# Four blocks of the up projection as seven products of quarter matrices in place of eight

## The chip, the core and the metric

The kernel runs on one core of a Trainium2 chip. The metric is the device time of one run in microseconds (us); less is better. The engines are named as the profile names them: PE (TensorE, matrix products) with PEld (the loading of its weights), DVE (VectorE), ACT (ScalarE), POOL (GpSimd) and SP (SyncE, which here issues DMA transfers). SBUF is the on-chip memory, PSUM the banks in which PE sums its products.

## The reference, cut to what matters

A block of a network: 512 tokens of 1024 values go through two mixers (a recurrent one and a sparse attention), a feed-forward stage with a short convolution, and a gated projection. All is float32. The change is in the feed-forward stage:

```python
def conv_ffn(h, w_up, conv_w, conv_b, w_down):
    u = h @ w_up                                  # [512,1024] @ [1024, 2*2048]
    gate, val = jnp.split(u, 2, axis=-1)
    gate = lax.conv_general_dilated(gate, ...) + conv_b   # width 3 along the tokens, each column by itself
    return (jax.nn.silu(gate) * val) @ w_down     # [512,2048] @ [2048,1024]
...
x = x + conv_ffn(rms_norm(x, ln2_g[i]), w_up[i], conv_w[i], conv_b[i], w_down[i])
```

`rms_norm` multiplies each token's row by one over its root mean square and each column by a gain.

## The kernel before, in words

Every large product is made of three products: both operands are split into a high part (rounded to the type fp32r, on ACT, tile names that end in h) and a low part (value minus high part, on DVE, names that end in l), and PE adds high x high, high x low and low x high in one PSUM bank (`gemm`, L443 to L452).

The feed-forward stage has 16 blocks f of 128 hidden columns. A block is two jobs: `wu{f}0` makes the gate rows, `wu{f}1` the value rows, each [128 columns x 512 tokens] over 1024 inputs in eight steps of 128, so 24 matmuls of 128x512 a job and 48 a block. The job's weight (128x1024) comes by a DMA into a tile that ends in r, ACT copies the high part (L166), DVE subtracts (L167). The class `Stream` works the list of jobs down: when a job begins it splits the next job's weight (`prepare(1)`). Raw, high and low weight tiles have two buffers each, and a new one is filled when the work that read the old one is done. The order of the instructions on each engine follows from data: an engine works its list in order, and the list is laid out by a scheduler from the program and the waits.

The inputs x2h and x2l are scaled by the gain alone. One over the root mean square of each token (the row `n2rb`) is multiplied in where the result leaves PSUM: `up_evac` (L1135 to L1153) makes zg from the gate's bank (DVE, times n2rb), three instructions of the convolution cv (ACT, DVE, DVE), the silu (ACT), zv from the value's bank (DVE, times n2rb), zv times cv (DVE), and the split of the result u (ACT high, DVE low). POOL has one 128x2 memset per block. After the 16 blocks the down projection reads U, whose four tiles hold four blocks each.

`xturn` is a tile of the down stage, `mixa`, `XH`, `XL` and `B16` are tags of large buffers that several stages use one after the other; `x2h` lies in XH and `x2l` in XL.

Of the kernel before, what the change touches and what calls it, by code (L numbers as in the profile page):

```python
# [19 lines left out]
NT = 4  # L20
# [38 lines left out]
C_G2, C_G3, C_GF = 0, 8, 16  # L59
C_CW, C_CB = 24, 72  # L60
# [8 lines left out]
def f32(ap):  # L69
    return ap.bitcast(F32)  # L70
# [3 lines left out]
def hybrid_block_kernel(ctx: ExitStack, tc: tile.TileContext, a, out):  # L74
    nc = tc.nc
    TE, VE, SE, GE = nc.tensor, nc.vector, nc.scalar, nc.gpsimd

    consts = ctx.enter_context(tc.tile_pool(name="consts", bufs=1))
    main = ctx.enter_context(tc.tile_pool(name="main", bufs=1))
    wpool = ctx.enter_context(tc.tile_pool(name="wpool", bufs=2))  # L80
# [20 lines left out]
    def pV(name):  # L101
        return bank("V", 1, 1, name)
# [7 lines left out]
    def t2k(name, dt=F32):  # L110
        return tmp.tile([128, 512], dt, tag="t2k", name=name)
# [37 lines left out]

    turn = [0]  # L150

    def load(name, src_ap, shape):
        raw = None
        if early[0]:
            turn[0] += 1
            if turn[0] % 6 < 4:
                raw = early[0][:, turn[0] % 6].rearrange("p (a b) -> p a b", a=shape[1])
        if raw is None:
            raw = wpool.tile(shape, F32, tag="raw", bufs=2, name=name + "r")
        nc.sync.dma_start(raw, src_ap)  # L160
# [21 lines left out]
    class Stream:  # L182


        def __init__(self):
            self.jobs, self.loaded, self.ready, self.cur, self.done = [], [], [], None, set()
            self.now, self.events, self.debt = 0.0, [], 0.0

        def add(self, name, src, shape, run):
            self.jobs.append((name, src, shape, run))  # L190

        def load(self, depth):
            while len(self.loaded) < depth and self.jobs:
                name, src, shape, run = self.jobs.pop(0)
                self.loaded.append((name, load(name, src, shape), shape, run))
                if name == "mv3":
                    early[0] = None

        def prepare(self, depth):
            while len(self.ready) < depth and (self.jobs or self.loaded):  # L200
                self.load(1)
                name, raw, shape, run = self.loaded.pop(0)
                self.ready.append((name, run, split(name, raw, shape)))

        def after(self, us, fn):
            self.events.append((self.now + us, len(self.events), fn))
# [49 lines left out]
    st = Stream()  # L256
# [211 lines left out]
    Q, vo, qk, X = {}, None, None, None  # L468
# [278 lines left out]
    mixa = main.tile([128, 2, 4, S], F32R, tag="mixa", name="mixa")  # L747
# [346 lines left out]
    x2h = main.tile([128, KB, S], F32R, tag="XH", name="x2h")  # L1094
    x2l = Halves("x2l")
# [5 lines left out]
    n2, n3 = {}, {}  # L1101

    def up_job(f, part):
        def run(wh, wl):
            ps = pW(f"pu{f}{part}")
            if f == 0:
                for k in range(KB):
                    triple(ps, wh, wl, k, x2h, x2l, k, k == 0, k == KB - 1)
                    yield 0.64
            else:  # L1110
                yield from gemm(ps, wh, wl, range(KB), x2h, x2l, range(KB))
            defer(n2, lambda: up_evac(f, part, ps, n2["rb"]))
        st.add(f"wu{f}{part}", a["w_up"][:, f, part], [128, KB, 128], run)

# [6 lines left out]
    def start_norm(norm, acc, name):  # L1121
        def stats():
            yc = rstd_stats(acc, name)
            if norm is n3:
                norm["yc"] = yc
                return
            st.after(T_NR, lambda: rows(yc))

        def rows(yc):
            norm["rb"] = rstd_rows(yc, name)  # L1130
            for fn in norm.get("pending", []):
                fn()
        st.after(T_NS, stats)

    def up_evac(f, part, ps, rb2):  # L1135
        if part == 0:
            zg = fpool.tile([128, S + 2], F32, name=f"zg{f}", tag="zg")
            GE.memset(zg[:, 0:2], 0.0)  # L1138
            VE.tensor_mul(zg[:, 2:S + 2], ps, rb2)  # L1139
            cw = lambda j: cols[:, C_CW + 16 * j + f:C_CW + 16 * j + f + 1]  # L1140
            cv = fpool.tile([128, S], F32, name=f"cv{f}", tag="cv")
            SE.activation(cv, zg[:, 2:S + 2], AF.Identity, scale=cw(2), bias=cols[:, C_CB + f:C_CB + f + 1])  # L1142
            VE.scalar_tensor_tensor(cv, zg[:, 1:S + 1], cw(1), cv, op0=ALU.mult, op1=ALU.add)  # L1143
            VE.scalar_tensor_tensor(cv, zg[:, 0:S], cw(0), cv, op0=ALU.mult, op1=ALU.add)  # L1144
            SE.activation(cv, cv, AF.Silu)  # L1145
            n2["cv"] = cv
# [134 lines left out]
    sa = pSa("pga")  # L1281
# [146 lines left out]
```

## Time and profile before

| | us |
|---|---|
| median of 3 runs (lowest to highest) | 629.54 (629.13 to 630.43) |
| the profiled run | 630.01 |
| its span, first to last instruction | 627.8 |
| PE busy in the span | 617.1 (98%) |
| DVE, ACT, POOL busy | 416.5 (66%), 315.9 (50%), 62.4 (10%) |
| granted TensorE clock, mean | 0.996 of full speed |

The chain that ended last is led by the last instructions of DVE (2% of the span); before them lies PE's work. The page's row of 40 slices shows PE at 9 tenths or more in all slices but the last. The feed-forward's up blocks begin at about 311 us. A duration in a row goes from the start of an instruction to its end; where instructions of an engine stand in a row, their starts are closer together than their durations, since one begins before the other has drained. The time that one costs its engine in a row is therefore read from start to start.

### The profile page before, as it was taken

The page shows a single profiled execution, that of the slowest core. Times are in us where ns is not written, and L with a number is a line of the kernel's source. Part 1 is how long each engine was busy: PE and PEld are TensorE (multiplying, and loading weights), DVE is VectorE, ACT ScalarE, POOL GpSimd, SP SyncE. Part 2 cuts the span into 40 slices and gives each one's busy share as a digit, 9 for nine tenths or more (in the row PEclk, how much of TensorE's full clock was granted, in tenths as well). Part 3 has the DMA queues.
Part 4 walks back from the last instruction along what each step waited for, and adds up shares of the span by engine and source line. Part 5 has one row for each costly group of instructions (what it writes and reads, how often), then busy time and mean ns, then how long its engine had stood idle before and what let it go on. Part 6 is the DMA issues. An engine that isn't in the chain of part 4 may idle for free. (4 is left out here: it accounts for less than half of the span.)

```text
span 627.8 us, 8441 instructions
## 1 busy us (share of the span) xinstructions
PE 617.1 (98%) x3021; PEld 500.7 (80%) x3021; DVE 416.5 (66%) x807; ACT 315.9 (50%) x663; POOL 62.4 (10%) x131
## 2 busy tenths in 40 slices
PE   9999999999999999999999999999999999999995
PEld 6888877777777777878888888888888888888784
DVE  6988757787777778882966665655556434345376
ACT  7455556677667766653744333334334223233254
POOL 0400009332333400000000000000000000000000
PEclk9999999999999999999999999999999999999998
DMA  8822136111221323022333322233333222534603
GB/s 304 306 64 70 36 103 157 42 37 66 68 68 34 132 71 101 34 69 67 101 101 100 102 86 90 92 101 101 101 101 101 96 89 85 165 103 138 185 14 135
DMA packets 23210, 63.04 MB, mean 100 GB/s; under 512 B 2744, under 2 KB 7736, under 8 KB 23100
## 3 DMA queue, kind: packets, MB, share of 16 engines
q1 hardware_dynamic: 21632, 59.93, 29.0%
q0 software_dynamic: 1248, 2.16, 1.5%
q8 instruction: 24, 0.39, 0.2%
q10 hardware_dynamic: 288, 0.41, 0.2%
q14 instruction: 18, 0.15, 0.1%
HBM read 56.72 MB, written 2.10 MB: 94 GB/s over the span
## 5 line engine op out<-in xcount | busy, mean ns | idle before, releaser
L808 POOL TENSOR_SCALAR E<-E,rr,sg 128x512 f32<-128x512 f32 (+3 forms) x54 | 38.3, 710 | 71.7 <-DVE rr L803 57.8
L1152 ACT ACTIVATE u<-zv 128x512 fp32r<-128x512 f32 x16 | 10.1, 634 | 45.0 <-DVE zv L1150 45.0
L837 DVE TENSOR_TENSOR pl<-pt,ph 128x512 fp32r<-128x512 f32 x40 | 27.2, 686 | 7.6 <-ACT ph L836 7.0
L1149 DVE TENSOR_TENSOR zv<-pu,n2rb 128x512 f32<-128x512 f32 x16 | 11.0, 691 | 31.0 <-PE pu L451 31.0
L836 ACT ACTIVATE ph<-pt 128x512 fp32r<-128x512 f32 x40 | 23.7, 600 | 15.4 <-PE pt L833 14.0
L1139 DVE TENSOR_TENSOR zg<-pu,n2rb 128x512 f32<-128x512 f32 x16 | 11.1, 692 | 26.0 <-PE pu L451 24.6
L833 PE MATMUL pt<-cols,E 128*128 128x128 f32 x160 | 26.4, 274 | 0.5 <-DVE E L808 0.4
L1138 POOL MEMSET zg<- 128x2 f32 x16 | 1.5, 99 | 244.0 <-DVE cv L1144 150.6
L1179 DVE TENSOR_TENSOR X<-pd,X 128x512 f32<-128x512 f32 x8 | 5.5, 692 | 29.6 <-PE pd L451 29.6
L833 PEld LDWEIGHTS pt<-cols,E 128*128 128x128 f32 x160 | 20.0, 140 | 6.3 <-DVE E L808 1.1
L1142 ACT ACTIVATE cv<-zg,cols 128x512 f32<-128x512 f32 x16 | 13.1, 817 | 20.1 <-DVE zg L1139 20.1
L1145 ACT ACTIVATE cv<-cv 128x512 f32<-128x512 f32 x16 | 10.1, 631 | 24.9 <-DVE cv L1144 24.9
L801 ACT ACTIVATE E<-s,nm 128x384 f32<-128x384 f32 (+2 forms) x48 | 22.1, 471 | 0.0
L841 PE MATMUL pv<-ph,V 128*128 128x512 f32 x40 | 18.9, 473 | 0.0
L1153 DVE TENSOR_TENSOR u<-zv,u 128x512 fp32r<-128x512 f32 x16 | 11.1, 692 | 10.5 <-ACT u L1152 10.5
L803 DVE RECIPROCAL rr<-rs 128x3 f32<-128x3 f32 x32 | 5.5, 172 | 16.9 <-ACT E L801 16.7
L843 PE MATMUL pv<-pl,V 128*128 128x512 f32 x40 | 16.5, 411 | 0.2 <-DVE pl L837 0.2
L791 DVE TENSOR_REDUCE nm<-s 128x2 f32<-128x768 f32 (+2 forms) x24 | 16.3, 680 | 0.0
L284 DVE TENSOR_TENSOR acc<-acc,sq 128x512 f32<-128x512 f32 x21 | 14.4, 684 | 0.1
L801 ACT ACTIVATE Ec<-s,nm 128x32 f32<-128x32 f32 x24 | 6.8, 283 | 13.5 <-DVE nm L791 10.4
L1144 DVE SCALAR_TENSOR_TENSOR cv<-zg,cols,cv 128x512 f32<-128x512 f32 x16 | 12.0, 751 | 0.5
L1143 DVE SCALAR_TENSOR_TENSOR cv<-zg,cols,cv 128x512 f32<-128x512 f32 x16 | 11.9, 746 | 0.2 <-issue 0.2
(1223 smaller groups left out, 2022.9 us busy)
## 6 DMA issues: line engine op xcount, KB each, us to landing
X<-in_xg SPq DMA_DIRECT2D x1, 2048.0 KB, 8.7
xo<-xturn SPq DMA_DIRECT2D x32, 64.0 KB, 2.0
wgr<-in_w_pg SPq DMA_DIRECT2D x4, 512.0 KB, 4.1
s1r<-in_w_s SPq DMA_DIRECT2D x3, 676.0 KB, 8.8
xT<-in_xg SPq DMA_DIRECT2D x3, 514.0 KB, 7.8
rawx<-in_w_mv SPq DMA_DIRECT2D x3, 512.0 KB, 6.5
Q<-hlq POOLq DMA_DIRECT2D x12, 128.0 KB, 3.1
out_y<-xo SPq DMA_DIRECT2D x3, 512.0 KB, 2.6
```

The lines of the kernel that those rows point to most:

```text
L284: return VE.tensor_add(acc[:, :n], acc[:, :n], sq[:, :n])
L791: VE.tensor_reduce(out=nm[:, 1:3], in_=sw, axis=AX.X, op=ALU.max, negate=True)
L801: SE.activation(e, p, AF.Exp, bias=nm[:, b:b + 1], accum_out=rs[:, b:b + 1])
L808: eng.tensor_scalar(e, e, rr[:, b:b + 1], sg[:, i, 3 * h + b:3 * h + b + 1], op0=ALU.mult, op1=ALU.mult)
L833: TE.transpose(pt[:, r * 128:(r + 1) * 128], Es[r][:, c0:c0 + 128], ident)
L836: SE.activation(ph, pt, AF.Copy)
L837: VE.tensor_sub(pl, pt, f32(ph))
L841: TE.matmul(pv, vs, ph, start=first, stop=False)
L843: TE.matmul(pv, vs, pl, start=False, stop=last)
L1142: SE.activation(cv, zg[:, 2:S + 2], AF.Identity, scale=cw(2), bias=cols[:, C_CB + f:C_CB + f + 1])
L1143: VE.scalar_tensor_tensor(cv, zg[:, 1:S + 1], cw(1), cv, op0=ALU.mult, op1=ALU.add)
L1144: VE.scalar_tensor_tensor(cv, zg[:, 0:S], cw(0), cv, op0=ALU.mult, op1=ALU.add)
```

## The change

Blocks 8, 9, 10 and 11 (`FAST`) are done by another formula. The product of a block, [2 x 128 columns] by [2 halves of the 1024 inputs] by [2 halves of the 512 tokens], is eight products of quarters; the changed kernel makes it of seven products of sums of quarters. Each is over 512 inputs in four steps and over 256 tokens: 12 matmuls of 128x256, so 84 a block.

- The sums of the inputs need inputs that are fully normalised: `scaled_input` makes xn (X times gain times n2rb), its high and low part xnh and xnl, one of eight pieces at a time while blocks 0 to 4 run, and POOL makes the sums tf (16 subtractions of 128x256). After block 4, `split_sums` splits them into th and tl. Blocks from 5 on read xnh and xnl, and no longer multiply by n2rb: zg is a copy by ACT, zv one DVE product less.
- The sums of the weights (`landed_b`) are made by POOL for each of the four blocks: four additions or subtractions of 128x512 into a tile `ws`, which has one buffer (the tag xturn). A block has four jobs: a (`wu{f}0`, gate weight, two products), b (`wu{f}s`, two sums), c (`wu{f}t`, two sums) and d (`wu{f}1`, half a weight, one product). So three splits of 128x1024 and one of 128x512 in place of two of 128x1024.
- The seven results are combined by a copy of ACT and seven additions of DVE over 256 columns. The convolution and the rest are as before, without n2rb.
- The four banks of blocks 8 and 10 are single tiles; blocks 9 and 11 take a two-bank tile (`pSa`) and two others.
- From before block 7 to the end of block 11 the weights are split two jobs ahead and loaded four ahead, and the raw tiles get two more buffers, the high and low ones one more each, from the feed-forward's pool.
- Two tiles move to other tags (x3h, gF, the last U), the attention's V tile is 130 in place of 132 wide for each head, and a scratch for DMA descriptors is 1024 in place of its default.

```diff
+FAST = (8, 9, 10, 11)
+UNSCALED = 5
+T_XN = 0.4, 5.4
+T_TS = 2.0, 5.4
+AHEAD = 4
 ...
+    turns = {}
+    def more(tag, n, extra, shape, dt, name):
+        if st.ahead:
+            turns[tag] = (turns.get(tag, -1) + 1) % (n + extra)
+            if turns[tag] >= n:
+                return fpool.tile(shape, dt, tag=tag, bufs=extra, name=name)
+        return wpool.tile(shape, dt, tag=tag, bufs=n, name=name)
 ...
-            raw = wpool.tile(shape, F32, tag="raw", bufs=2, name=name + "r")
+            raw = more("raw", 2, 2, shape, F32, name + "r")
 ...
-        hi = wpool.tile(shape, F32R, tag="hi", name=name + "h")
-        lo = wpool.tile(shape, F32R, tag="lo", name=name + "l")
+        hi = more("hi", 2, 1, shape, F32R, name + "h")
+        lo = more("lo", 2, 1, shape, F32R, name + "l")
 ...
-                self.prepare(1)
+                self.prepare(self.depth)
+                self.load(self.ahead)
 ...
-    VW = 4 * 132
+    VW = 4 * 130
 ...
+            elif f < UNSCALED:
+                yield from gemm(ps, wh, wl, range(KB), x2h, x2l, range(KB))
             else:
-                yield from gemm(ps, wh, wl, range(KB), x2h, x2l, range(KB))
+                yield from gemm(ps, wh, wl, range(KB), xnh, xnl, range(KB))
+                up_evac(f, part, ps, None)
+                return
 ...
+            for q, b in enumerate((0, 4, 1, 5, 2, 6, 3, 7)):
+                st.after(T_XN[0] + T_XN[1] * q, lambda b=b: scaled_input(b))
 ...
-            VE.tensor_mul(zg[:, 2:S + 2], ps, rb2)
+            zg = gate_rows(f)
+            if rb2 is None:
+                SE.activation(zg[:, 2:S + 2], ps, AF.Copy)
+            else:
+                VE.tensor_mul(zg[:, 2:S + 2], ps, rb2)
+            convolve(f, zg)
         else:
             zv = fpool.tile([128, S], F32, name=f"zv{f}", tag="zv")
-            VE.tensor_mul(zv, ps, rb2)
+            if rb2 is None:
+                VE.tensor_mul(zv, ps, n2["cv"])
+            else:
+                VE.tensor_mul(zv, ps, rb2)
+                VE.tensor_mul(zv, zv, n2["cv"])
+            hidden(f, zv)
 ...
+    def scaled_input(b):
+        xn = t2k(f"xn{b}")
+        i = VE.scalar_tensor_tensor(xn, X[:, b], cols[:, C_G2 + b:C_G2 + b + 1], n2["rb"], op0=ALU.mult, op1=ALU.mult)
+        SE.activation(xnh[:, b], xn, AF.Copy)
+        VE.tensor_sub(xnl[:, b], xn, f32(xnh[:, b]))
+        n2["xn", b] = xn
+        if b >= 4:
+            j = b - 4
+            top = n2["xn", j]
+            b11, b12, b21, b22 = top[:, 0:H], top[:, H:], xn[:, 0:H], xn[:, H:]
+            t1, t2, t3, t4 = (Tf[:, j, q] for q in range(4))
+            GE.tensor_sub(t1, b12, b11)
+            GE.tensor_sub(t3, b22, b12)
+            GE.tensor_sub(t2, b22, t1)
+            GE.tensor_sub(t4, b21, t2)
 ...
+    def split_sums(j):
+        SE.activation(Th[:, j], Tf[:, j], AF.Copy)
+        VE.tensor_sub(Tl[j // 2][:, j % 2], Tf[:, j], f32(Th[:, j]))
+    def seven(ps, w, x):
+        (wh, wl), (rh, rl) = w, x
+        for j in range(4):
+            TE.matmul(ps, wh[:, j], rh(j), start=j == 0, stop=False)
+            TE.matmul(ps, wh[:, j], rl(j), start=False, stop=False)
+            yield 0.24
+        for j in range(4):
+            TE.matmul(ps, wl[:, j], rh(j), start=False, stop=j == 3)
+            yield 0.12
+    def quarter(k0, t0):
+        return (lambda j: xnh[:, k0 + j, t0:t0 + H]), (lambda j: xnl[:, k0 + j, t0:t0 + H])
+    def tsum(q):
+        return (lambda j: Th[:, j, q]), (lambda j: Tl[j // 2][:, j % 2, q])
 ...
+    def fast_banks(f):
+        fast_turn[0] += 1
+        if fast_turn[0] % 2:
+            ps = [pG(f"pfa{f}"), pT(f"pfb{f}"), pG(f"pfc{f}"), pT(f"pfd{f}")]
+        else:
+            sa = pSa(f"pfa{f}")
+            ps = [sa[:, 0], sa[:, 1], pSb(f"pfc{f}"), pV(f"pfd{f}")]
+        return [p[:, t0:t0 + H] for p in ps for t0 in (0, H)]
+    def up_fast(f):
+        d = {}
+        half = lambda w, q: (w[0][:, 4 * q:4 * q + 4], w[1][:, 4 * q:4 * q + 4])
+        def landed_a(raw):
+            d["r0"] = raw
+        def landed_b(raw):
+            r0, d["r1"] = d["r0"], raw
+            sums = fpool.tile([128, 2, 8, 128], F32, bufs=1, name=f"ws{f}", tag="xturn")
+            s2, s1, s3, s4 = sums[:, 0, 0:4], sums[:, 0, 4:8], sums[:, 1, 0:4], sums[:, 1, 4:8]
+            GE.tensor_add(s1, raw[:, 0:4], raw[:, 4:8])
+            GE.tensor_sub(s2, s1, r0[:, 0:4])
+            GE.tensor_sub(s3, r0[:, 0:4], raw[:, 0:4])
+            GE.tensor_sub(s4, r0[:, 4:8], s2)
+            d["sums"] = sums
+        def prep_b(name, raw, shape):
+            return split(name, d["sums"][:, 0], shape)
+        def prep_c(name, raw, shape):
+            return split(name, d["sums"][:, 1], shape)
+        def prep_d(name, raw, shape):
+            return split(name, d["r1"][:, 4:8], shape)
+        def run_a(wh, wl):
+            d["ps"] = fast_banks(f)
+            d["u"] = t2k(f"fu{f}")
+            d["v"] = t2k(f"fv{f}")
+            p1, p2 = d["ps"][0:2]
+            yield from seven(p1, half((wh, wl), 0), quarter(0, 0))
+            v1 = d["v"][:, H:]
+            yield from seven(p2, half((wh, wl), 1), quarter(4, 0))
+            SE.activation(v1, p1, AF.Copy)
+            d["zg"] = gate_rows(f)
+            VE.tensor_add(d["zg"][:, 2:2 + H], p2, v1)
+        def run_b(wh, wl):
+            p1, p2, p6, p5 = d["ps"][0:4]
+            u2, u4 = d["u"][:, 0:H], d["v"][:, 0:H]
+            yield from seven(p6, half((wh, wl), 0), tsum(1))
+            yield from seven(p5, half((wh, wl), 1), tsum(0))
+            VE.tensor_add(u2, p6, d["v"][:, H:])
+            VE.tensor_add(u4, p5, u2)
+        def run_c(wh, wl):
+            p5, p7, p3 = d["ps"][3:6]
+            u2, u3, u4 = d["u"][:, 0:H], d["u"][:, H:], d["v"][:, 0:H]
+            d["zv"] = fpool.tile([128, S], F32, name=f"zv{f}", tag="zv")
+            yield from seven(p7, half((wh, wl), 0), tsum(2))
+            yield from seven(p3, half((wh, wl), 1), quarter(4, H))
+            VE.tensor_add(d["zg"][:, 2 + H:], p3, u4)
+            convolve(f, d["zg"])
+            VE.tensor_add(u3, p7, u2)
+            VE.tensor_add(d["zv"][:, H:], p5, u3)
+        def run_d(wh, wl):
+            zv, p4 = d["zv"], d["ps"][6]
+            yield from seven(p4, (wh, wl), tsum(3))
+            VE.tensor_add(zv[:, 0:H], p4, d["u"][:, H:])
             VE.tensor_mul(zv, zv, n2["cv"])
+            hidden(f, zv)
 ...
+        full = [128, KB, 128]
+        st.add(f"wu{f}0", a["w_up"][:, f, 0], full, run_a, landed=landed_a)
+        st.add(f"wu{f}s", a["w_up"][:, f, 1], full, run_b, prep_b, landed_b)
+        st.add(f"wu{f}t", None, full, run_c, prep_c)
+        st.add(f"wu{f}1", None, [128, 4, 128], run_d, prep_d)
 ...
-    U = [fpool.tile([128, 2, 4, S], F32R, name="u0", bufs=1),
-         main.tile([128, 2, 4, S], F32R, tag="B16", bufs=3, name="u1"),
-         main.tile([128, 2, 4, S], F32R, tag="B16", bufs=3, name="u2"),
-         main.tile([128, 2, 4, S], F32R, tag="mixa", name="u3")]
+    U = [fpool.tile([128, 2, 4, S], F32R, name="u0", bufs=1)]
+    xnh = main.tile([128, KB, S], F32R, tag="mixa", name="xnh")
+    xnl = fpool.tile([128, KB, S], F32R, bufs=1, tag="xo", name="xnl")
+    Tf = main.tile([128, 4, 4, H], F32, tag="B16", bufs=3, name="tf")
+    U.append(main.tile([128, 2, 4, S], F32R, tag="B16", bufs=3, name="u1"))
+    st.until(f"wu{UNSCALED - 1}1")
+    Th = main.tile([128, 4, 4, H], F32R, tag="XH", name="th")
+    Tl = [main.tile([128, 2, 4, H], F32R, tag=f"XL{h}", name=f"tl{h}") for h in range(2)]
+    for j in range(4):
+        st.after(T_TS[0] + T_TS[1] * j, lambda j=j: split_sums(j))
+    st.until(f"wu{min(FAST) - 2}1")
+    st.depth, st.ahead = 2, AHEAD
+    st.until("wu71")
+    U.append(main.tile([128, 2, 4, S], F32R, tag="B16", bufs=3, name="u2"))
+    st.until("wu111")
+    U.append(main.tile([128, 2, 4, S], F32R, tag="XH", name="u3"))
+    st.depth, st.ahead = 1, 0
     st.until("wu151")
-    xo = fpool.tile([128, NT, 2, 512], F32, bufs=1, name="xo")
-    x3h = main.tile([128, KB, S], F32R, tag="XH", name="x3h")
+    xo = fpool.tile([128, NT, 2, 512], F32, bufs=1, tag="xo", name="xo")
+    x3h = main.tile([128, KB, S], F32R, tag="mixa", name="x3h")
     x3l = Halves("x3l")
 ...
-    nc = _bacc.Bacc("TRN2", target_bir_lowering=False, num_devices=1)
+    nc = _bacc.Bacc("TRN2", target_bir_lowering=False, num_devices=1, dynamic_dma_scratch_size=1024)
```

On PE, before, one block's value job is followed by the next block's gate job, with a low part (l) at the end of each (pu: the bank; wu101: value weight of block 10).

```order
L448 MATMUL pu_4262<-x2lb,wu101h 128x512
L451 MATMUL pu_4262<-x2h,wu101l 128x512 x8
L447 MATMUL pu_4298<-x2h,wu110h 128x512
L448 MATMUL pu_4298<-x2la,wu110h 128x512
L447 MATMUL pu_4298<-x2h,wu110h 128x512
```

On PE, after, in block 11 (pfa: the two-bank tile of products a and b, pfc and pfd: the banks of products c and d; wu11s, wu11t: the sums of job b and c):

```order
L1225 MATMUL pfd_4549<-th,wu111h 128x256
L1226 MATMUL pfd_4549<-tl_3893,wu111h 128x256
L1229 MATMUL pfc_4548<-th,wu11tl 128x256 x4
L1225 MATMUL pfc_4548<-xnh,wu11th 128x256
L1226 MATMUL pfc_4548<-xnl,wu11th 128x256
L1225 MATMUL pfc_4548<-xnh,wu11th 128x256
L1226 MATMUL pfc_4548<-xnl,wu11th 128x256
L1225 MATMUL pfa_4547<-th,wu11sh 128x256
```

Here products d and c stand ahead of b: six of job d's matmuls, then the low part of c, then b's first. In blocks 8 and 10 the order is a, b, c, d; in block 9 it is as here, with one matmul of d ahead of c's low part.

On DVE, before, from one block's value to the next one's convolution (u: low part of the result):

```order
L167 TENSOR_TENSOR wu81l<-wu81r,wu81h 128x1024
L1150 TENSOR_TENSOR zv_4062<-zv_4062,cv_4026 128x512
L1153 TENSOR_TENSOR u_3435<-zv_4062,u_3435 128x512
L1139 TENSOR_TENSOR zg_4098<-pu_4073,n2rb 128x512
L167 TENSOR_TENSOR wu90l<-wu90r,wu90h 128x1024
L1143 SCALAR_TENSOR_TENSOR cv_4101<-zg_4098,cols,cv_4101 128x512
L1144 SCALAR_TENSOR_TENSOR cv_4101<-zg_4098,cols,cv_4101 128x512
```

On DVE, after, from block 8's second half of the gate to block 9's first (fu, fv: places for the partial sums):

```order
L1301 TENSOR_TENSOR zg_4180<-pfc_4151,fv_4154 128x256
L1303 TENSOR_TENSOR fu_4153<-pfc_4151,fu_4153 128x256
L182 TENSOR_TENSOR wu9sl<-ws_4110,wu9sh 128x1024
L1169 SCALAR_TENSOR_TENSOR cv_4245<-zg_4180,cols,cv_4245 128x512
L1304 TENSOR_TENSOR zv_4219<-pfb_4150,fu_4153 128x256
L1170 SCALAR_TENSOR_TENSOR cv_4245<-zg_4180,cols,cv_4245 128x512
L1309 TENSOR_TENSOR zv_4219<-pfd_4152,fu_4153 128x256
L182 TENSOR_TENSOR wu9tl<-ws_4110,wu9th 128x1024
L1310 TENSOR_TENSOR zv_4219<-zv_4219,cv_4245 128x512
L1285 TENSOR_TENSOR zg_4313<-pfa_4283,fv_4287 128x256
```

The low parts of the sums wu9s and wu9t now stand between the additions, the convolution and the product of block 8; wu9t's, which PE needs early in block 9, stands behind the last addition of block 8, which reads the product d.

## Rows read from the trace of the kernel before

**Rows 1.** The page, busy time, its share and instructions of each engine
```profile
PE 617.1 (98%) x3021; PEld 500.7 (80%) x3021; DVE 416.5 (66%) x807; ACT 315.9 (50%) x663; POOL 62.4 (10%) x131
```
**Rows 2.** Waits of PE: engine, line, waited for, us in all, times, longest
```profile
PE idle L141 <- DVE ones L266: 1.2, 1, 1.2
PE pmt L1063 <- ACT num L1056: 0.5, 2, 0.3
```
**Rows 3.** Timeline of PE, first matmul of three weights: start, us, engine, line, tiles
```profile
421.44 0.39 PE L447 MATMUL pu<-x2h,wu100h 128*128 128x512 f32 x1
...
426.88 0.39 PE L447 MATMUL pu<-x2h,wu101h 128*128 128x512 f32 x1
...
432.32 0.39 PE L447 MATMUL pu<-x2h,wu110h 128*128 128x512 f32 x1
```
**Rows 4.** Timeline of PE near the end: first and 25th of half-width matmuls
```profile
614.36 0.28 PE L1318 MATMUL pg<-wres,x3h 128*128 128x256 f32 x1
...
617.23 0.28 PE L1318 MATMUL pg1last<-wres,x3h 128*128 128x256 f32 x1
```
**Rows 5.** Windows of the up stage: stretch, length, busy us (instructions) by engine
```profile
323.50:367.00 43.50, 43.50 (x193) 36.05 (x192) 27.27 (x35) 19.95 (x24) 0.50 (x5) 1.00 0.30 97
399.00:443.00 44.00, 44.00 (x196) 36.45 (x195) 25.43 (x32) 16.71 (x21) 0.40 (x4) 1.00 0.29 96
421.44:432.32 10.88, 10.88 (x49) 9.01 (x48) 6.36 (x8) 4.10 (x5) 0.10 (x1) 1.00 0.29 97
```
**Rows 6.** Timeline of DVE and ACT over one block; idle before in brackets
```profile
405.33 0.69 DVE L1139 TENSOR_TENSOR zg<-pu,n2rb 128x512 f32<-128x512 f32 x1 [1.62 <-PE pu L451]
405.94 1.22 DVE L167 TENSOR_TENSOR wu90l<-wu90r,wu90h 128x1024 fp32r<-128x1024 f32 x1
406.05 0.82 ACT L1142 ACTIVATE cv<-zg,cols 128x512 f32<-128x512 f32 x1 [1.43 <-DVE zg L1139]
407.07 0.74 DVE L1143 SCALAR_TENSOR_TENSOR cv<-zg,cols,cv 128x512 f32<-128x512 f32 x1
407.85 0.75 DVE L1144 SCALAR_TENSOR_TENSOR cv<-zg,cols,cv 128x512 f32<-128x512 f32 x1
408.63 0.63 ACT L1145 ACTIVATE cv<-cv 128x512 f32<-128x512 f32 x1 [1.76 <-DVE cv L1144]
409.17 1.04 ACT L166 ACTIVATE wu91h<-wu91r 128x1024 fp32r<-128x1024 f32 x1
410.77 0.69 DVE L1149 TENSOR_TENSOR zv<-pu,n2rb 128x512 f32<-128x512 f32 x1 [2.17 <-PE pu L451]
411.37 1.22 DVE L167 TENSOR_TENSOR wu91l<-wu91r,wu91h 128x1024 fp32r<-128x1024 f32 x1
412.51 0.69 DVE L1150 TENSOR_TENSOR zv<-zv,cv 128x512 f32<-128x512 f32 x1
```
**Rows 7.** Timeline of POOL and DVE in the attention stage, three meetings
```profile
93.46 0.79 POOL L808 TENSOR_SCALAR E<-E,rr,sg 128x512 f32<-128x512 f32 x1
...
94.22 0.36 POOL L808 TENSOR_SCALAR Ec<-Ec,rr,sg 128x32 f32<-128x32 f32 x1
...
94.39 1.48 DVE L475 TENSOR_TENSOR hlq<-zq,hlq 128x512 fp32r<-128x512 f32 x1
94.56 0.76 POOL L808 TENSOR_SCALAR E<-E,rr,sg 128x512 f32<-128x512 f32 x1
...
100.93 0.79 POOL L808 TENSOR_SCALAR E<-E,rr,sg 128x512 f32<-128x512 f32 x1
101.15 0.68 DVE L579 SCALAR_TENSOR_TENSOR zq<-pq,n1rb 128x512 f32<-128x512 f32 x1
...
165.50 0.45 POOL L808 TENSOR_SCALAR E<-E,rr,sg 128x128 f32<-128x128 f32 x1 [2.03 <-DVE rr L803]
...
166.28 1.22 DVE L167 TENSOR_TENSOR mq3l<-mq3r,mq3h 128x1024 fp32r<-128x1024 f32 x1
166.28 1.53 POOL L808 TENSOR_SCALAR E<-E,rr,sg 128x128 f32<-128x128 f32 x1
```

More of the change, by code (lines that the diff above doesn't have):

```diff
@@ L186, in __init__, with add @@
             self.jobs, self.loaded, self.ready, self.cur, self.done = [], [], [], None, set()
-            self.now, self.events, self.debt = 0.0, [], 0.0
-        def add(self, name, src, shape, run):
-            self.jobs.append((name, src, shape, run))
+            self.now, self.events, self.debt, self.depth, self.ahead = 0.0, [], 0.0, 1, 0
+        def add(self, name, src, shape, run, prep=split, landed=None):
+            self.jobs.append((name, src, shape, run, prep, landed))
         def load(self, depth):
             while len(self.loaded) < depth and self.jobs:
-                name, src, shape, run = self.jobs.pop(0)
-                self.loaded.append((name, load(name, src, shape), shape, run))
+                name, src, shape, run, prep, landed = self.jobs.pop(0)
+                raw = load(name, src, shape) if src is not None else None
+                if landed:
+                    landed(raw)
+                self.loaded.append((name, raw, shape, run, prep))
                 if name == "mv3":
@@ L201, in prepare @@
                 self.load(1)
-                name, raw, shape, run = self.loaded.pop(0)
-                self.ready.append((name, run, split(name, raw, shape)))
+                name, raw, shape, run, prep = self.loaded.pop(0)
+                self.ready.append((name, run, prep(name, raw, shape)))
         def after(self, us, fn):
@@ L596, in q_evac @@
         return evac
-    VW = 4 * 132
+    VW = 4 * 130
     def vones(j, h):
-        return vo[:, j * VW + h * 132:j * VW + h * 132 + 130]
+        return vo[:, j * VW + h * 130:j * VW + (h + 1) * 130]
     def mv_done():
@@ L1132, in rows, with gate_rows, convolve @@
                 fn()
+            for q, b in enumerate((0, 4, 1, 5, 2, 6, 3, 7)):
+                st.after(T_XN[0] + T_XN[1] * q, lambda b=b: scaled_input(b))
         st.after(T_NS, stats)
+    def gate_rows(f):
+        zg = fpool.tile([128, S + 2], F32, name=f"zg{f}", tag="zg")
+        GE.memset(zg[:, 0:2], 0.0)
+        return zg
+    def convolve(f, zg):
+        cw = lambda j: cols[:, C_CW + 16 * j + f:C_CW + 16 * j + f + 1]
+        cv = fpool.tile([128, S], F32, name=f"cv{f}", tag="cv")
+        SE.activation(cv, zg[:, 2:S + 2], AF.Identity, scale=cw(2), bias=cols[:, C_CB + f:C_CB + f + 1])
+        VE.scalar_tensor_tensor(cv, zg[:, 1:S + 1], cw(1), cv, op0=ALU.mult, op1=ALU.add)
+        VE.scalar_tensor_tensor(cv, zg[:, 0:S], cw(0), cv, op0=ALU.mult, op1=ALU.add)
+        SE.activation(cv, cv, AF.Silu)
+        n2["cv"] = cv
@@ L1135, in up_evac, with hidden @@
+    def hidden(f, zv):
+        uh, ul = U[f // 4][:, 0, f % 4], U[f // 4][:, 1, f % 4]
+        SE.activation(uh, zv, AF.Copy)
+        VE.tensor_sub(ul, zv, f32(uh))
     def up_evac(f, part, ps, rb2):
         if part == 0:
-            zg = fpool.tile([128, S + 2], F32, name=f"zg{f}", tag="zg")
-            GE.memset(zg[:, 0:2], 0.0)
-            VE.tensor_mul(zg[:, 2:S + 2], ps, rb2)
-            cw = lambda j: cols[:, C_CW + 16 * j + f:C_CW + 16 * j + f + 1]
-            cv = fpool.tile([128, S], F32, name=f"cv{f}", tag="cv")
@@ L1142, in up_evac @@
[L1142 to L1146, printed above, removed]
+            zg = gate_rows(f)
[3 more added lines that the diff above has]
+                VE.tensor_mul(zg[:, 2:S + 2], ps, rb2)
@@ L1147, in up_evac @@
+            convolve(f, zg)
         else:
             zv = fpool.tile([128, S], F32, name=f"zv{f}", tag="zv")
-            VE.tensor_mul(zv, ps, rb2)
-            VE.tensor_mul(zv, zv, n2["cv"])
-            uh, ul = U[f // 4][:, 0, f % 4], U[f // 4][:, 1, f % 4]
-            SE.activation(uh, zv, AF.Copy)
-            VE.tensor_sub(ul, zv, f32(uh))
+            if rb2 is None:
[3 more added lines that the diff above has]
+                VE.tensor_mul(zv, zv, n2["cv"])
@@ new lines, in up_evac @@
+            hidden(f, zv)
+    H = S // 2
+    def scaled_input(b):
[13 more added lines that the diff above has]
+            GE.tensor_sub(t4, b21, t2)
@@ new lines, in quarter @@
+    def quarter(k0, t0):
+        return (lambda j: xnh[:, k0 + j, t0:t0 + H]), (lambda j: xnl[:, k0 + j, t0:t0 + H])
+    def tsum(q):
+        return (lambda j: Th[:, j, q]), (lambda j: Tl[j // 2][:, j % 2, q])
+    fast_turn = [0]
+    def fast_banks(f):
[6 more added lines that the diff above has]
+        return [p[:, t0:t0 + H] for p in ps for t0 in (0, H)]
@@ L1188, in hybrid_block_kernel @@
     for f in range(16):
+        if f in FAST:
+            up_fast(f)
+            continue
         for part in range(2):
@@ L1206, in hybrid_block_kernel @@
     st.drain()
-    gF = main.tile([128, 2, 512], F32, tag="mixa", name="gF")
+    gF = main.tile([128, 2, 512], F32, tag="XH", name="gF")
     nc.sync.dma_start(gF, a["gF"])
```

## The prediction, made before the changed kernel had run

> **What bounds the kernel now.** First the page's busy times: PE has 617.1 us of work in a span of 627.8, 98% [rows 1]. Then PE's waits: the longest is 1.2 us at the very start, the next line has 0.5 [rows 2]. So PE does not wait, and the kernel is as long as its products. Third, the windows of the up stage: from 399 to 443 PE is busy for all of 44.00 us at the full clock (1.00), DVE for 25.43, ACT for 16.71, POOL for 0.40 [rows 5]. DVE and ACT have room, and what they do there costs nothing. Last, the timeline of a block shows that room: DVE waits 1.62 us for PE before zg and 2.17 before zv, and ACT waits for DVE [rows 6]. The change spends it, so the question is whether the room holds what is put in.
>
> The profiled run took 630.01 us, 2.2 more than its span and 0.47 above the median of 629.54. I add and subtract on the profiled run and take 0.47 off at the end.
>
> **What it removes: PE's time.** From wu100's first matmul to wu110's are two jobs, 48 matmuls of 128x512: 432.32 - 421.44 = 10.88 us, 0.2267 each [rows 3]. At half width the trace has 24 matmuls from 614.36 to 617.23, 2.87 us, 0.1196 each [rows 4]; they load a new weight each too. A block of seven products is 84 x 0.1196 = 10.05 us, 0.83 less. Four blocks: 3.33 us. With nothing lost the profiled run would be 626.7 and the median 626.2.
>
> **What it adds to DVE and ACT.** Cost in a row is read from start to start [rows 6]: a 128x1024 split 1.13 (405.94 to 407.07), a 128x512 product 0.61 (405.33 to 405.94), one of the convolution 0.78 (407.07 to 407.85). A 256-wide addition has no row there; by the slope between 512 and 1024 it is 0.61 - 0.26 = 0.35. A fast block is three splits and a half one (3.39 + 0.61), seven additions (2.45), two of the convolution (1.56), a product and a low part (1.22): 9.23 us of DVE in 10.05. The same count of a block before gives 2.26 + 1.56 + 2.44 = 6.26, where the window has 6.36 [rows 5], so the count holds. ACT: three high parts of 1.04 and a half, 0.82 and 0.63 for cv, a 256-wide copy and u, some 6.3 of 10.05. Both fit if nothing else holds them.
>
> **What POOL's sums add.** Four operations of 128x512 a block, each with two inputs and an output in SBUF. That meets DVE. Three places show how [rows 7]. At 166.28 a POOL operation of 128x128 that otherwise takes 0.45 took 1.53 beside a split of DVE of 1.22, which reads SBUF twice. At 94.39 DVE's hlq, of two SBUF inputs and 512 wide, took 1.48 where such a one takes 0.69 [rows 6], beside two operations of POOL. At 101.15 a DVE operation that reads PSUM took 0.68, and POOL's beside it 0.79, its usual. So one holds the other up only where DVE has two SBUF inputs, and then one runs after the other. Of a fast block's 9.23, all but the seven additions from PSUM are of that kind: 9.23 - 2.45 = 6.8 us. With four sums of d each, 6.8 + 4d must fit into 10.05, so d must be 0.81 or less.
>
> The trace has no two-input operation on POOL. From below: 0.77, the one-input row at 512. From above: the second input costs as much as the first operand; the slope from 0.45 at 128 to 0.77 at 512 is 0.32, so 0.43 for 512, and the sum 1.2. If it cost a whole operation more it would be 1.54. I take 0.95, between the first two and nearer to the measured row. The Trainium skill speaks against it: "GPSIMD Engine Reference", section "3.1 Elementwise — side-by-side cycle accounting", has a two-input addition of 2048 elements at 4497 ns, nearly twice DVE's; an estimate from it and the row's fixed part of about 0.33 is 0.33 + 4.17 / 4 = 1.37. No row here shows it. By it the sum would be 633.0, in the upper part of the third rival.
>
> The sums for block 8 fall into block 7, where DVE has room; those for 9, 10 and 11 fall into fast blocks. Three blocks at 6.8 + 4d - 10.05: for 0.77 nothing, for 0.95 0.55 each and 1.65 in all, for 1.2 1.55 and 4.65. The weights prepared two jobs ahead are a lead of up to 2.87 us against that; the waits within a queue, where what stands behind a held instruction could have gone, weigh on the other side. I let these two cancel, which is the softest step here.
>
> **The order in blocks 9 and 11.** Since a and b share a two-bank tile, c's and d's matmuls stand before b's. Block 9's low part wu9tl is wanted after 24 + 8 + 1 matmuls, 3.95 us into the block, not after 56 (6.70). DVE: block 8's c product ends 1.44 before block 9 begins, DVE starts some 0.21 after a product (zg at 405.33, where wu81's first matmul by three jobs of 5.44 back from 421.44 was at 405.12). Then zg and fu (0.70), wu9sl (1.13), cv, zv, cv (1.91), zv (0.35), wu9tl (1.13): ready at -1.23 + 5.22 = 3.99. No room at all, and 0.05 lost, with nothing of POOL in between. For block 11 it is 38 matmuls, 4.54, with 0.5 of room. I add 0.1.
>
> **The rest.** While blocks 0 to 4 run, eight pieces of xn cost DVE 0.78 + 0.61 each, 11.1 us in a stretch that has 43.50 - 27.27 = 16.2 free [rows 5]. POOL's 16 sums of half width (0.56 by the slope, up to 0.77) are 9 to 12 more that partly shut DVE out, and it can be some 2 us late; but the low part wu90l, ready at 407.07, is wanted at 410.56 + 16 x 0.2267 = 414.2, so 7 us of room cover it. Without them it would cost those 2. The four splits of tf (1.13 each) are spread over blocks 5 and 6, where zv loses one DVE product and zg goes to ACT, 1.22 a block back. The loads are the same bytes; buffers, tags, the V tile and the scratch I put at nothing, between -0.3 and +0.5, as no wait in rows 2 names them.
>
> **Sum.** 630.01 - 3.33 + 1.65 + 0.1 = 628.4, less 0.47: 627.9.
>
> **Rivals.**
> 1. All is hidden: POOL's sums are short (0.8 or less), or the lead covers the overrun. Then 626.2 to 626.7. For it: DVE idles over 40% of the up stage now [rows 5]. Against it: 0.81 is only just above the one-input row.
> 2. Preparing xn stalls PE: sums and splits collide through the first five blocks and a weight comes late by more than its 7 us, or ACT's queue holds a weight's high part behind a piece of xn. That costs 1.5 to 3 beside the 1.75 of the sum: 629.4 to 631. Against it: the room just named.
> 3. It ends slower: POOL's sums are long, and POOL and DVE in turn become the bound of blocks 8 to 10. Mechanism: an operation waits for the other engine's, the low parts of the sums come late, PE waits for them at the start of b and c, above all in 10 and 11. It eats the gain from 3 x (4d - 3.25) = 3.2, d = 1.08; at 1.2 the time is 626.2 + 4.65 + 0.1 = 631.0, at 1.37, midway to 1.54, 6.7 is lost and it is 633.0; at 1.54 it is 635.0. For it: hlq's 1.48 and POOL's 1.53 [rows 7]; against it: the lead, and that DVE's idle times before zg and zv [rows 6] show in which order the two meet matters.
>
> **How the numbers follow.** The forecast (d from 0.85 to 1.1, 626.8 to 629.8): 0.38, of which 0.30 is faster by over 0.2% and 0.08 within. Two tenths of a per cent are 1.3 us, about what a measurement of this kernel can tell from no change, so from 628.3 to 630.8 is no change. Rival 1: 0.12, faster. Rival 2: 0.15, of it 0.03 faster, 0.09 within, 0.03 slower. Rival 3: 0.35, 0.08 within and 0.27 slower. Together 0.45 faster, 0.25 the same, 0.30 slower. The range goes from 626.0 to 632.8; what is left out is rival 3 with d above 1.35.
>
> **What would show it.** The first matmuls of blocks 8 to 11 should be 10.05 apart plus waits, plain blocks 10.88. A POOL sum alone should take 0.95; if it takes 1.2 or more, rival 3 has its price. DVE's splits should stretch beside POOL's sums to 1.5 to 2. PE's waits, none now, should be at the low parts of the sums, late in the four blocks and most in block 11. Waits between 323 and 389 would speak for rival 2; a saving of 3.3 with no waits for rival 1. The forecast is wrong if half-width matmuls do not keep 0.12, or if the waits of blocks 8 to 11 add up to over 3.3.

## The result, and the profile after

The changed kernel takes 633.12 us (median of 5 runs, 632.76 to 633.51), the kernel before 629.29 beside it: a ratio of 1.0056, 95% interval 1.0045 to 1.0067. It is 3.8 us slower where 1.6 us faster was forecast, and the range ended at 632.8. The profiled run took 633.06, its span is 631.3.

The page's busy times, to hold against [rows 1]:

```profile
PE 617.3 (98%) x3165; PEld 505.5 (80%) x3165; DVE 446.2 (71%) x841; ACT 334.8 (53%) x694; POOL 108.4 (17%) x163
```

PE is busy for as long as before, though four blocks have an eighth less to do. That is the first surprise: something has made other work longer. The waits of PE, to hold against [rows 2]:

```profile
PE pfa L1229 <- DVE wu110l L182: 1.5, 1, 1.5
PE pfc L1229 <- DVE wu11tl L182: 1.4, 1, 1.4
PE idle L146 <- DVE ones L285: 1.2, 1, 1.2
PE pmt L1082 <- ACT num L1075: 0.4, 2, 0.3
PE pu L460 <- DVE wu01l L182: 0.4, 1, 0.4
```

Three are new, 3.3 us: two in block 11 and one in block 0. So waits explain the lost gain and not the 3.8 us beyond it. Where the rest lies is seen from the first matmuls of the jobs in PE's timeline, to hold against [rows 3]:

```profile
367.30 0.39 PE L466 MATMUL pu<-xnh,wu50h 128*128 128x512 f32 x1
...
371.00 0.39 PE L470 MATMUL pu<-xnh,wu50l 128*128 128x512 f32 x1
...
372.81 0.39 PE L466 MATMUL pu<-xnh,wu51h 128*128 128x512 f32 x1
...
378.33 0.39 PE L466 MATMUL pu<-xnh,wu60h 128*128 128x512 f32 x1
...
400.42 0.28 PE L1225 MATMUL pfa<-xnh,wu80h 128*128 128x256 f32 x1
...
410.41 0.28 PE L1225 MATMUL pfa<-xnh,wu90h 128*128 128x256 f32 x1
...
420.39 0.28 PE L1225 MATMUL pfa<-xnh,wu100h 128*128 128x256 f32 x1
...
430.37 0.28 PE L1225 MATMUL pfa<-xnh,wu110h 128*128 128x256 f32 x1
...
444.42 0.39 PE L466 MATMUL pu<-xnh,wu120h 128*128 128x512 f32 x1
```

Read the distances. Block 5's jobs take 5.51 and 5.52 us, where a job took 5.44: PE waits for nothing there, the count of matmuls and the clock (1.00) are the same, and still each job is 1.4% longer. Blocks 8, 9 and 10 take 9.99, 9.98 and 9.98 us, a little under the 10.05 of the forecast. Block 11 takes 14.05.

The whole difference, by the first matmuls of both traces (before, after):

| stretch | before | after | difference |
|---|---|---|---|
| up to wu00 | 310.80 | 310.35 | -0.45 |
| wu00 to wu10 (block 0) | 12.70 | 13.40 | +0.70 |
| wu10 to wu50 | 43.54 | 43.54 | 0 |
| wu50 to wu80 (blocks 5 to 7) | 32.64 | 33.12 | +0.48 |
| wu80 to wu120 (the fast four) | 43.51 | 44.00 | +0.49 |
| wu120 to wd00 (blocks 12 to 15) | 43.52 | 44.24 | +0.72 |
| wd00 to wd70 (seven of eight down blocks) | 77.00 | 78.03 | +1.03 |
| from wd70 to the last matmul | 56.27 | 56.69 | +0.42 |

The sum is +3.4; the spans differ by 3.5. The first line is of no weight: over the runs below other than e5 wu00 began anywhere from 308.8 to 309.7 us after the first matmul. The fast four hold 4 x (10.88 - 9.98) = 3.6 of gain and 14.05 - 9.98 = 4.1 of loss, all in block 11: the two waits, 2.9 as the view counts them, and what PE loses in stopping and starting (two shorter pauses, and after each of four stops the second matmul starts 0.22 us behind the first in place of 0.12). The lines of longer jobs hold 0.48 + 0.72 + 1.03 + 0.42 = 2.65.

Beside block 10's end, DVE and POOL in turn (timeline of the two engines):

```profile
426.75 1.66 POOL L1260 TENSOR_TENSOR ws<-wu11sr 128x512 f32<-128x512 f32 x1 [1.33 <-DVE wu10tl L182]
427.52 1.45 DVE L182 TENSOR_TENSOR wu101l<-wu10sr,wu101h 128x512 fp32r<-128x512 f32 x1
428.38 1.75 POOL L1262 TENSOR_TENSOR ws<-wu110r,wu11sr 128x512 f32<-128x512 f32 x1
428.90 0.41 DVE L1292 TENSOR_TENSOR fu<-pfb,fv 128x256 f32<-128x256 f32 x1
429.23 1.45 DVE L1177 TENSOR_TENSOR u<-zv,u 128x512 fp32r<-128x512 f32 x1
430.08 1.75 POOL L1261 TENSOR_TENSOR ws<-ws,wu110r 128x512 f32<-128x512 f32 x1
430.60 0.41 DVE L1293 TENSOR_TENSOR fv<-pfb,fu 128x256 f32<-128x256 f32 x1
430.93 1.97 DVE L182 TENSOR_TENSOR wu110l<-wu110r,wu110h 128x1024 fp32r<-128x1024 f32 x1
431.90 2.15 POOL L1263 TENSOR_TENSOR ws<-wu110r,ws 128x512 f32<-128x512 f32 x1
```

DVE's 512-wide low parts take 1.45 in place of 0.69 and the split wu110l 1.97 in place of 1.22 [rows 6]. wu110l ends at 432.90; PE's matmul that reads it starts at 432.96. The additions from PSUM (0.41) are not held.

The first row shows something else. `ws` has one buffer, so POOL begins block 11's sums only when DVE's wu10tl has read block 10's, and all four fall beside the low parts that block 11 needs. No run gave `ws` a second buffer; how much of the loss one would give back is open.

And in block 0, where nothing was expected:

```profile
314.13 1.29 POOL L1260 TENSOR_TENSOR ws<-wu8sr 128x512 f32<-128x512 f32 x1 [3.37 <-DMA wu8sr<-in_w_up]
314.51 1.99 DVE L182 TENSOR_TENSOR wu01l<-wu01r,wu01h 128x1024 fp32r<-128x1024 f32 x1
```

POOL makes block 8's first sum 86 us early, as soon as its weight has landed. DVE's split comes 0.38 later, is held, and block 0 loses 0.7. The price asked for, that of a sum alone, is seen in block 7, where POOL makes block 8's second sum; DVE is idle for its first 1.0 us and then reads PSUM:

```profile
388.64 1.30 POOL L1261 TENSOR_TENSOR ws<-ws,wu80r 128x512 f32<-128x512 f32 x1 [1.25 <-DMA wu80r<-in_w_up]
389.64 0.69 DVE L1191 TENSOR_TENSOR zv<-pu,cv 128x512 f32<-128x512 f32 x1 [2.50 <-PE pu L470]
```

It takes 1.30, and the one at 314.13, which nothing held either, 1.29.

### The profile page after: what moved, and what is told of

It is laid out like the page before. It is cut to its first block, busy times and chain, and to the rows that moved or that the text cites. A ratio compares the mean times of both kernels' runs of the same rounds, so it can differ in the third digit from the quotient of the medians.

```text
span 631.3 us, 8839 instructions
## 1 busy us (share of the span) xinstructions
PE 617.3 (98%) x3165; PEld 505.5 (80%) x3165; DVE 446.2 (71%) x841; ACT 334.8 (53%) x694; POOL 108.4 (17%) x163
## 4 chain that ended last, share of the span: by engine, by line
PE 85%; DVE 9%; ACT 2%; issue 2%; POOL 1%; DMA 1%; DVEq 0%; ACTq 0%; POOLq 0%
PE pu L467 6%; PE pu L466 6%; PE pu L470 6%; PE pd L467 5%; PE pd L466 5%; PE pd L470 5%; PE pt L852 2%; PE ptm L413 2%; PE pmq L470 2%; PE pmq L466 2%; PE pmq L467 2%; PE pc L417 2%; PE pv L860 2%; PE pv L862 1%; PE mo L1053 1%
## 5 line engine op out<-in xcount | busy, mean ns | idle before, releaser
L1169 DVE SCALAR_TENSOR_TENSOR cv<-zg,cols,cv 128x512 f32<-128x512 f32 x16 | 13.4, 839 | 3.9 <-ACT cv L1168 3.9
L498 POOL DMA_DIRECT2D Q<-hlq x12 | 6.3, 540 | 54.9 <-ACT hlq L493 54.9
L1191 DVE TENSOR_TENSOR zv<-pu,cv 128x512 f32<-128x512 f32 x7 | 4.8, 691 | 15.2 <-PE pu L470 14.5
L1177 DVE TENSOR_TENSOR u<-zv,u 128x512 fp32r<-128x512 f32 x16 | 13.9, 868 | 1.1 <-ACT u L1176 1.1
L1170 DVE SCALAR_TENSOR_TENSOR cv<-zg,cols,cv 128x512 f32<-128x512 f32 x16 | 12.4, 776 | 0.2
```

## The experiments

Theory A: POOL's sums and DVE shut each other out, and the low parts of the weights come late. Rival B: the order a, c, d, b makes the waits. Theory C: a 128x512 matmul's pace depends on where the moving tile lies relative to the weight tile, modulo 256 bytes. Its grounds are the addresses that the programs give their tiles: in the program before, weight tiles and all big moving tiles lie at 160 modulo 256, except U's first tile (192); after, weights lie at 32, xnl and U's first tile at 64, two other U tiles at 160. All of the jobs that read these are the longer ones; x2h, x2l (32) kept 5.44.

**e1, no weight sums**

```diff
-            GE.tensor_add(s1, raw[:, 0:4], raw[:, 4:8])    # and the other three
-            return split(name, d["sums"][:, 0], shape)
+            return split(name, d["r1"], shape)             # job c: d["r0"]
```

> The changed kernel with POOL's four weight sums of each block left out: jobs b and c split the loaded weights themselves (so the four blocks' values are not the reference's), all else as it is. Theory A, that POOL's sums and DVE shut each other out and the low parts of the sums come late: block 11 takes 10.0 us like 8 to 10 in place of 14.05, and the wait of 0.7 us at wu01l, where the first sum stood beside DVE's split, goes too: 633.1 - 4.0 - 0.7 = 628.4 us. Rival B, that the order a, c, d, b of blocks 9 and 11 makes the waits: the 1.4 to 1.7 us at wu11tl stay and the time is 630 us.

628.78 us; ratio to the kernel before 0.9983 (0.9974 to 0.9992), so 0.73% or 4.6 us better than the changed kernel. Block 11 takes 10.19 us, blocks 8 to 10 as before, block 0 12.87, and no wait for a low part is left:

```profile
429.89 0.28 PE L1225 MATMUL pfa<-xnh,wu110h 128*128 128x256 f32 x1
...
440.08 0.39 PE L466 MATMUL pu<-xnh,wu120h 128*128 128x512 f32 x1
```

Theory A expected 4.7 us; the ratios give 4.6, the traces 4.4 (3.86 in block 11 and 0.53 in block 0). Leaving out the sums takes away their lateness along with their holding of DVE, so the total alone does not say which of the two it is. DVE's rows do, here without the sums and then in the changed kernel:

```profile
425.77 0.68 DVE L182 TENSOR_TENSOR wu101l<-wu10sr,wu101h 128x512 fp32r<-128x512 f32 x1
...
427.96 1.21 DVE L182 TENSOR_TENSOR wu110l<-wu110r,wu110h 128x1024 fp32r<-128x1024 f32 x1
...
433.19 1.21 DVE L182 TENSOR_TENSOR wu11tl<-wu110r,wu11th 128x1024 fp32r<-128x1024 f32 x1
```

```profile
437.56 1.22 DVE L182 TENSOR_TENSOR wu11tl<-ws,wu11th 128x1024 fp32r<-128x1024 f32 x1
```

From wu101l's start to wu11tl's end DVE has the same 13 operations in the same order. They take 8.63 us here and 11.26 (427.52 to 438.78) beside the sums, with 0.4 idle in either: the 2.6 between is held time. The order a, c, d, b alone costs no more than the 0.2 us of block 11. The long jobs are still there (wu50 to wu51: 5.52).

**e2, the same four single banks in each fast block**

```diff
-        if fast_turn[0] % 2:
             ps = [pG(f"pfa{f}"), pT(f"pfb{f}"), pG(f"pfc{f}"), pT(f"pfd{f}")]
-        else:
-            sa = pSa(f"pfa{f}")
-            ps = [sa[:, 0], sa[:, 1], pSb(f"pfc{f}"), pV(f"pfd{f}")]
```

> The changed kernel with the same four single banks in every fast block, so that blocks 9 and 11 also run a, b, c, d. Rival B: no wait at wu11tl, 1.4 to 2 us less, 631.1 to 631.7. Theory A: the sums come as late as before and the wait moves to the start of b in block 11 or 10; the time is 632 to 633.5, no more than 1 us better.

631.64 us, ratio 1.0029 (1.0017 to 1.0041): 1.7 us better, as rival B had it, and more than A allowed. But the wait is not gone, it has moved:

```profile
PE pfb L1225 <- DVE zv L1299: 1.7, 2, 1.2
```

Block 10 takes 10.72 and block 11 11.75; PE waits at b for a bank that a late DVE has not read yet. With e1: the lag is POOL's and DVE's; the banks, and the order that follows from them, decide how much of it reaches PE, 4.1 us or 2.5.

**e3, tiles moved, nothing else**

```diff
-    VW = 4 * 130
+    VW = 4 * 132
     fpool = ctx.enter_context(tc.tile_pool(name="fpool", bufs=2))
+    fpool.tile([128, 56], F32, name="pad0", bufs=1)
-dynamic_dma_scratch_size=1024
+dynamic_dma_scratch_size=768
```

> The changed kernel with all moving tiles of the feed-forward at the same place modulo 256 bytes as the weight tiles (the attention's V tile back to 132 a head, 224 bytes of padding ahead of the feed-forward's pool, 768 bytes of descriptor scratch in place of 1024); no instruction added or taken out. Theory C, that a 128x512 matmul costs 227 ns where moving tile and weight tile agree modulo 256 bytes and 231 to 236 where they differ: blocks 5 to 7 and 12 to 15 go back to 5.44 us a job (1.2 us), the down stage and the last stage lose their 1.6 us, and U's first tile, which was off in the kernel before too, gives 0.9: 633.1 - 3.7 = 629.4 us (629.4 to 630.4). Rival: what is slow is the tiles' distance or the other engines' traffic; then no change, 633.1.

629.83 us, ratio 1.0002 (0.9993 to 1.0011): 3.4 us better with not one instruction more or less. The jobs' first matmuls:

```profile
367.94 0.39 PE L466 MATMUL pu<-xnh,wu50h 128*128 128x512 f32 x1
...
373.38 0.39 PE L466 MATMUL pu<-xnh,wu51h 128*128 128x512 f32 x1
...
378.82 0.39 PE L466 MATMUL pu<-xnh,wu60h 128*128 128x512 f32 x1
```

5.44 again. From wd00 to wd70 it is 76.16 us (78.03 in the changed kernel, 77.00 before). The waits of block 11 stay, 1.4 and 1.4, and the block takes 14.01. Blocks 12 to 15 take 43.70, 0.18 over the kernel before: wu120 lies in an extra weight buffer that the padding left at 224.

**e4, the kernel before with U's first tile moved**

```diff
     fpool = ctx.enter_context(tc.tile_pool(name="fpool", bufs=2))
+    fpool.tile([128, 56], F32, name="pad0", bufs=1)
```

> The kernel before with 224 bytes of padding ahead of the feed-forward's pool, which puts U's first tile at the weights' place modulo 256 bytes. Theory C: the first half of each job wd{b}0 goes from 232 to 227 ns a matmul, 0.11 us a job, eight jobs: 629.3 - 0.9 = 628.4 us. Rival (distance or traffic): 629.3, no change.

629.16 us, ratio 0.9992 (0.9983 to 1.0001): -0.5 us, with an interval from -1.1 to +0.1. The time alone would not settle it; the trace does. The first jobs of the down stage, in the kernel before and then here:

```profile
486.73 0.40 PE L447 MATMUL pd<-u,wd00h 128*128 128x512 f32 x1
...
492.29 0.39 PE L447 MATMUL pd<-u,wd01h 128*128 128x512 f32 x1
...
497.73 0.40 PE L447 MATMUL pd<-u,wd10h 128*128 128x512 f32 x1
```

```profile
486.09 0.39 PE L447 MATMUL pd<-u,wd00h 128*128 128x512 f32 x1
...
491.53 0.39 PE L447 MATMUL pd<-u,wd01h 128*128 128x512 f32 x1
...
496.97 0.39 PE L447 MATMUL pd<-u,wd10h 128*128 128x512 f32 x1
```

wd00, which reads U's first tile, goes from 5.56 us to 5.44; wd01, which does not, keeps 5.44. From wd00 to wd70 it is 76.16 in place of 77.00, -0.84 over seven blocks.

**e5 and e6, the kernel before with all weights moved by 128 or 256 bytes**

```diff
+    padp = ctx.enter_context(tc.tile_pool(name="padp", bufs=1))
+    padp.tile([128, 32], F32, name="padw")      # e6: 64
     wpool = ctx.enter_context(tc.tile_pool(name="wpool", bufs=2))
```

> The kernel before with 128 bytes of padding between the big tiles and the weight pool, so that every weight tile is 128 bytes off the moving tiles modulo 256; no instruction changed. Theory C (place modulo 256 bytes): the up jobs of 5.44 us go to 5.5 to 5.6 (230 to 234 ns a matmul), 0.06 to 0.16 for each of 32, and other stages as well: 634 to 640 us. Rival C2 (it is the distance of the tiles or which pool they lie in): no change, 629.8.

> The same with 256 bytes of padding. Theory C: the up jobs stay at 5.44 us and the time is that of the kernel before, 629.8 (U's first tile keeps its place modulo 256, so the down stage keeps its 77.0 us from wd00 to wd70). Rival C3 (any shift of the weights costs, or the modulus is larger than 256): slower like the shift by 128.

By 128: 636.68 us, ratio 1.0107 (1.0092 to 1.0123), inside theory C's range. By 256: 630.11, ratio 1.0005 (0.9996 to 1.0014). PE's timeline with the shift of 128:

```profile
369.69 0.39 PE L449 MATMUL pu<-x2h,wu50h 128*128 128x512 f32 x1
...
375.26 0.39 PE L449 MATMUL pu<-x2h,wu51h 128*128 128x512 f32 x1
...
380.85 0.40 PE L449 MATMUL pu<-x2h,wu60h 128*128 128x512 f32 x1
```

5.57 and 5.59 us a job. With 256 a block takes 10.88 and wd00 to wd70 77.00, as before. In e5 the moving tiles of the up blocks agree with each other and only the weights are off, so the pair that counts is moving tile and weight. The pool is ruled out by e5 (the same pool, and slower), the distance by e6 (another distance, and the same pace).

**e7 and e8, the fast blocks apart**

```diff
-FAST = (8, 9, 10, 11)
+FAST = (7, 8, 10, 11)                           # e8: (7, 9, 11)
-            GE.tensor_add(s1, raw[:, 0:4], raw[:, 4:8])
+            first = GE.tensor_add(s1, raw[:, 0:4], raw[:, 4:8])
+            if f == FAST[0]:
+                behind(first, lows[f"wu{f - 2}1"], "not beside the first blocks", wait=True)
```

with the edits of e2 and e3.

> Tiles placed as in e3, single banks in every fast block as in e2, the fast blocks at 7, 8, 10 and 11 with the plain block 9 between, and the first weight sum held back until block 5's value weight is split. Theory A: the plain block gives POOL and DVE time to catch up, so block 8 and 11 wait little (0 to 1 us) and each fast block saves 0.85: 629.8 - 0.9 (U's first tile) - 3.4 + 0.5 = 626.0 us (625.4 to 627). If it is not the accumulated lag but each fast block by itself, the waits of 1.5 to 2 stay: 628.

> As e7 with three fast blocks, 7, 9 and 11, each behind a plain one. Theory A: the sums of each fall into a plain block, no wait for them at all: 629.8 - 0.9 - 2.6 = 626.3 us. If the lag is per block, 627 to 628.

e7: 625.50 us, ratio 0.9934 (0.9922 to 0.9946), the fastest of all, 4.2 us under the kernel before. Of these, U's first tile is 0.5 by e4's time and 0.84 by its trace, and the kernel before can have that too. e8: 625.83, ratio 0.9940 (0.9927 to 0.9952). In e7:

```profile
387.98 0.28 PE L1225 MATMUL pfa<-xnh,wu70h 128*128 128x256 f32 x1
...
398.00 0.28 PE L1225 MATMUL pfa<-xnh,wu80h 128*128 128x256 f32 x1
...
408.00 0.40 PE L466 MATMUL pu<-xnh,wu90h 128*128 128x512 f32 x1
...
418.91 0.28 PE L1225 MATMUL pfa<-xnh,wu100h 128*128 128x256 f32 x1
...
428.91 0.28 PE L1225 MATMUL pfa<-xnh,wu110h 128*128 128x256 f32 x1
...
439.37 0.40 PE L466 MATMUL pu<-xnh,wu120h 128*128 128x512 f32 x1
```

Fast blocks of 10.02, 10.00, 10.00 and 10.46, and a plain one of 10.91 between; block 0 is back at 12.72. In e8 the three fast blocks take 10.02 each without a wait, but the plain ones between take 11.06 in place of 10.88. Their gate weights lie in the extra buffer at 224, 64 off, their value weights at 160, in place; in PE's timeline of e8 the two jobs of one block stand side by side:

```profile
398.33 0.40 PE L466 MATMUL pu<-xnh,wu80h 128*128 128x512 f32 x1
...
403.94 0.39 PE L466 MATMUL pu<-xnh,wu81h 128*128 128x512 f32 x1
...
409.39 0.28 PE L1225 MATMUL pfa<-xnh,wu90h 128*128 128x256 f32 x1
```

5.61 us with the weight off, 5.45 with it in place, from the same inputs. The lag adds up over blocks in a row, and a plain block takes it back: the third fast block costs 10.72 in a row with the others (e2) and 10.00 behind the plain one (e7). e7 and e8 make several edits at once, so what each edit gives of their time is not shown apart.

## Why the prediction was wrong

1. *What bounds the kernel, and what is saved on PE*: right. A fast block without waits takes 9.98 to 10.02 us against 10.05.
2. *The price of a sum, d = 0.95*: this step failed. Free of DVE it takes 1.29 to 1.30 (314.13, 388.64; in e7 three more). The bound of 1.2 was passed; the upper one of 1.54 holds. The figure of the Trainium skill ("GPSIMD Engine Reference", section "3.1 Elementwise — side-by-side cycle accounting") that was set aside gave 1.37 as an estimate, and the trace sides with it: 1.29 is nearer to 1.37 than to 0.95.
3. *The loss from sharing, 3 x (6.8 + 4d - 10.05)*: the mechanism is right (e1), its size in part. The sum had 1.65 for it; with d = 1.29 it would be 5.7; measured are 4.1. The weights prepared ahead may count for the 1.6 between; no run took that apart, nor the one buffer of `ws`, for which the sum had no term. The forecast let that lead and the waits in the queues cancel. All of it came in block 11, as the text had it.
4. *The sums for block 8 fall into block 7*: wrong for the first of the four. POOL made it at 314, beside block 0's split, for 0.7 us; held back in e7, it leaves block 0 at 12.72. Nothing in the program held it back here, and an idle POOL took what had landed.
5. *The order of blocks 9 and 11, 0.1 us*: nothing was lost in block 9. In block 11 the order alone costs 0.2 at most (e1), but with the lag the loss was 4.1, where the other banks and order have 2.5 (e2).
6. *xn in blocks 0 to 4*: right, no wait of PE between 323 and 399. DVE was busy for 42.15 of 43.50 us (27.27 before, [rows 5]), and the room of 7 us covered it.
7. *Buffers, tags, the V tile and the scratch at nothing, between -0.3 and +0.5*: this step failed too, by 2.65 us (e3). None of them adds an instruction, but they set where tiles lie. [rows 3] could not show it; the down stage of the kernel before could have, where the jobs that read U's first tile took 5.56 us and the others 5.44 (e4).

Steps 2 to 5 alone: -3.6 + 4.1 + 0.7 = +1.2. Step 7 adds 2.65: 3.85 in all, against 3.8 of the medians and 3.5 of the spans. The time of 633.0 that the third rival had for d = 1.37 is near the measured one by two errors that cancel: too much loss from sharing, and none from placement.

## What to carry to other kernels

Before work is given to an idle POOL, count what DVE reads twice from SBUF in the same stretch: the two must fit one after the other, and leave plain work between such stretches so that the lag does not add up. When tiles, tags or buffers move, compare the pace of matmuls that the change does not touch, by the starts of two jobs, before and after; 1.4% on such jobs cost 2.65 us here, most of the saving of 3.6. A saving on the engine that sets the time is real only after both have been looked at: with both mended, the same idea gave 4.2 us, 0.5 to 0.84 of it from U's first tile alone.

## What the runs showed of the hardware that was not expected

A 128x512 matmul of this kernel costs 227 ns (5.44 us for 24) where its moving tile and its weight tile lie at the same place modulo 256 bytes in SBUF, and 232 to 234 on average where they differ by 64 (e8's wu80, 5.61 / 24) or 128 (e5, 5.57 / 24). A shift by 256 changes nothing. Where two moving tiles take turns and one is off, the matmuls are slower on average: in wu50 of the changed kernel the 16 matmuls that read xnh and xnl in turn take 3.70 us (367.30 to 371.00, 231 ns each), the 8 that read xnh alone 1.81 (226 each). Why it is so the runs do not say. Matmuls of 128x256 do not gain from it: a fast block takes 9.99 with xnl off (the changed kernel) and 10.02 with it in place (e3).
